# A hybrid attention and SSM layer in float32 on one core: the second half's output projection as seven block products, with weight sums and a scaled input made on GpSimd

## The chip, the cores and the metric

The kernel runs on one core of a Trainium2 chip. The metric is the device time of one execution in microseconds, as a median over runs: 2883.91 us over 3 runs (2882.71 to 2888.22) for the kernel before.

## The reference

A layer takes x (1 x 2048 x 2048, float32) and computes, cut to what matters:

```
h = rms_norm(x, norm_w)
q, k, v, z_attn, u, z_ssm = split(h @ w_in)            # 1024, 256, 256, 1024, 1024, 1024 columns
o_attn = sliding_window_attention(q, k, v, sinks) * silu(z_attn)   # window 128, 16 heads, 4 kv heads
y = gelu(s5_ssm(u, ...)); y = y * sigmoid(y @ w_glu + b_glu)
o_ssm = y * silu(z_ssm)
merged = concat(rms_norm(o_attn, attn_out_norm_w), rms_norm(o_ssm, ssm_out_norm_w))
out = x + merged @ w_out                               # w_out is 2048 x 2048
```

## The kernel before

Every large matrix product is done in three float32r matmuls: each operand is split into a high part (a cast on ScalarE) and a low part (a subtraction on VectorE), and high x high, high x low and low x high are summed in PSUM. The sequence is worked in two halves of 1024 tokens (HT). The activations of a half lie transposed in SBUF as 16 pairs of tiles xh0 to xh15 and xl0 to xl15 (128 x 1024). Weights come through a pool of three buffers each: wr (as loaded, 256 KB), wh and wl (its parts).

The panels are of two kinds. panel_feat (matmul at L331, 512 columns wide, 24 matmuls per weight unit) makes u, z_attn and z_ssm; panel_tok (L349, 256 columns, 48 matmuls per unit) makes q, k, v and the first half's output projection. A third, out_wide (L966), makes the second half's output projection: for four groups of 512 output columns it runs over the attention half and then the SSM half of the 2048 inputs, 8 weight units each, with 8 token tiles and 3 matmuls per tile, 1536 matmuls of 512 columns in all. The row scales of the two norms (ra, rss) are applied per token when PSUM is read out.

The order of the work is written as Python generators: weave runs a list of panels and draws a number of steps of a side generator between them. In turn:

- first u panels of half 0, then u, k, v, q and z_attn of half 0 (6, 6 and 8 panels, 104 weight units), woven with setup_all: rope tables, row statistics of half 1 (x_stats), and ssm_setup, whose last part fills four tables Ct and St on VectorE, one per step, in the pool "tb";
- z_ssm of half 0, then x_later, which loads x of half 1, scales it by the row scale (spread over columns by spread, a set of small matmuls at L281) and by norm_w, and splits it; then u of half 1; woven with attention of half 0 (attend_all, attend: 16 pairs of 128-query blocks, two passes of two heads in each block);
- z_attn, q, k, v, z_ssm of half 1 woven with the SSM itself (ssm_pairs);
- glu of half 0, the output projection of half 0 (out_panel) woven with attention of half 1, glu of half 1 with tail_attn at its side (loads the attention output, splits it, sums its squares), and out_wide.

The steps give a program order; the instruction scheduler of the framework then sets the order on each engine by its own estimate of times and by priorities. All bulk transfers are issued from one queue, SyncE's (SP). That queue is in order too: a store that waits for an engine holds back every load behind it. The staged tiles oa, ob, sz, xq, xr and zt share four buffers of 512 KB.

In attend, a row of scores holds 256 keys of two blocks; only 128 of them are in the window, and they are folded into one 128-wide tile by a mask. The probabilities ph and pl (high and low part, transposed) are multiplied by two masks sel (previous block and own block) into pm, and four matmuls (L562) of pm against the value blocks give the output. The masks of ph run on GpSimd (POOL), those of pl on VectorE.

Of the kernel before, what the change touches and what calls it, by code (L numbers as in the profile page):

```python
# [20 lines left out]
P = 128  # L21
# [20 lines left out]
class Hymba:  # L42
    def __init__(self, ctx, tc, a, out, dbg):
# [25 lines left out]
        self.QS = d("QS", [SEQ, 1024])  # L69
        self.xh, self.xl = [None] * NK, [None] * NK  # L70
# [83 lines left out]
    def consts(self):  # L154
# [11 lines left out]
        self.sel = c.tile([P, 2, P], F32, tag="sel", name="sel")  # L166
        nc.gpsimd.memset(self.sel, 1.0)
        nc.gpsimd.affine_select(out=self.sel[:, 0], in_=self.sel[:, 0], pattern=[[-1, P]],
                                compare_op=ALU.is_gt, fill=0.0, base=0, channel_multiplier=1)
        nc.gpsimd.affine_select(out=self.sel[:, 1], in_=self.sel[:, 1], pattern=[[1, P]],  # L170
# [126 lines left out]
    def x_later(self, half, pool):  # L297

        nc = self.nc
        rb = pool.tile([P, HT], F32, tag="rb", name="rb")  # L300
        self.spread(self.rstd[:, half * 8:half * 8 + 8], rb, pool)
        for k in range(NK):
            x = self.stage("xq")
            self.ld.dma_start(x, self.a["xT"][k * P:(k + 1) * P, half * HT:half * HT + HT])
# [204 lines left out]
    def attend(self, pool, half, g, bq0, kst, vst, zT, qst):  # L509
        nc = self.nc  # L510
        oT = pool.tile([P, 2, 256], F32, tag="oT", name="oT", bufs=2)
        for bq in range(bq0, bq0 + 2):
# [3 lines left out]
            for hp in range(2):  # L516
# [18 lines left out]
                for h in range(2):  # L535
                    self.stt(negm[:, h:h + 1], mx[:, h:h + 1], nrs[:, h:h + 1], nsk[:, h:h + 1], ALU.mult, ALU.min)
# [7 lines left out]
                self.tt(sm, sm, bc(den.unsqueeze(2), (P, 2, P)), ALU.mult)  # L544
# [8 lines left out]
                if b:  # L553
                    pm = pool.tile([P, 2, 2, 256], F32R, tag="pm", name="pm", bufs=2)
                    for i, (pp, eng) in enumerate(((ph, nc.gpsimd), (pl, nc.vector))):
                        for kb in range(2):
                            self.tt(pm[:, i, kb].rearrange("p (h q) -> p h q", h=2), pp.bitcast(F32).rearrange("p (h q) -> p h q", h=2),
                                    bc(self.sel[:, kb].unsqueeze(1), (P, 2, P)), ALU.mult,
                                    eng)
                    for i in range(2):  # L560
                        for kb in range(2):
                            nc.tensor.matmul(po, vst[:, blk + kb, :], pm[:, i, kb], start=(i == 0 and kb == 0),  # L562
                                             stop=(i == 1 and kb == 1))
# [9 lines left out]
            if blk:  # L573
                self.tt(oT, oT, zT, ALU.mult)
                t0 = (b - 1) * P
                self.st.dma_start(self.OA[g * 256:g * 256 + 256, t0:t0 + 256].rearrange("(c p) t -> p c t", p=P), oT)
# [3 lines left out]
    def ssm_setup(self):  # L580
# [162 lines left out]
        with ExitStack() as es:  # L743
            pool = es.enter_context(self.tc.tile_pool(name="tb", bufs=1))
            for bt in range(4):
# [22 lines left out]
                yield  # L768
# [119 lines left out]

    def glu_in(self, half, pool, k0):
# [13 lines left out]
    def glu(self, half, pool, yin, side, k0):  # L903
# [26 lines left out]
        for _ in side:  # L930
            pass
        for m in range(8):
# [23 lines left out]

    def out_wide(self, n):

        nc = self.nc
        for i, k0 in enumerate((0, 8)):  # L960
            ps = [self.psg() if t < 4 else self.psa() for t in range(8)]
            for k in range(8):
                hi, lo = self.w_unit(self.a["w_out"], i * 1024 + k * P, 1, n * 512, 512)
# [172 lines left out]
```

## Time and profile before

| | |
|---|---|
| median of 3 runs | 2883.91 us |
| the profiled execution | 2888.56 us |
| its span on the core | 2886.8 us, mean granted TensorE clock 0.992 |
| TensorE matmuls | 2801.0 us busy (97%), 16992 |
| VectorE, ScalarE, GpSimd | 1897.9, 961.3, 205.0 us busy |

A span is the time from the first to the last instruction on the core. The busy time of TensorE is the union of its matmuls; as they overlap, the pace of a stretch is better read as its length divided by its matmuls. Times of stages below are microseconds from the start of the span.

### The profile page before, as it was taken

To read this page: it belongs to the slowest core of one execution; us is meant where nothing else is said; L and a number is where in the kernel's file an instruction comes from. 1 tells how busy PE (TensorE), PEld (TensorE's weight loads), DVE (VectorE), ACT (ScalarE), POOL (GpSimd) and SP (SyncE) were. 2 spreads that over 40 slices of the span, in tenths; PEclk is the share of its full clock that TensorE was granted. 3 is DMA by queue.
4 is the path that set the end of the run, shared out by engine and by line. 5 is a ranking of instruction groups with operands and counts; after the bars stand their busy time and mean duration, and the time that the engine had idled before them with its cause. 6 is when DMAs were issued, how large, how long until landed. Compare 5 with 4: busy or idle time off the path is not lost.

```text
span 2886.8 us, 45269 instructions
## 1 busy us (share of the span) xinstructions
PE 2801.0 (97%) x16992; PEld 2502.2 (87%) x16992; DVE 1897.9 (66%) x4419; ACT 961.3 (33%) x2089; POOL 205.0 (7%) x341
## 2 busy tenths in 40 slices
PE   6989999989999899999999999998999999999999
PEld 5879999878888688888999988878999999778887
DVE  6682746856773976677679985378999884842222
ACT  6421212134442543333323332345444433521110
POOL 0000000001110112000000000000222220000000
PEclk9999999999999999999999999999999999999999
DMA  5842536553332532544355555343444436333321
GB/s 175 237 117 69 158 92 168 142 142 112 94 115 75 183 115 84 159 144 146 120 156 148 154 156 145 101 138 96 136 143 124 124 106 186 107 104 106 106 78 57
DMA packets 421290, 369.34 MB, mean 128 GB/s; under 512 B 53200, under 2 KB 377296, under 8 KB 421072
## 3 DMA queue, kind: packets, MB, share of 16 engines
q1 hardware_dynamic: 419008, 366.45, 42.9%
q8 instruction: 134, 2.20, 0.3%
q14 instruction: 84, 0.69, 0.1%
q10 hardware_dynamic: 2064, 0.01, 0.0%
HBM read 271.03 MB, written 99.55 MB: 128 GB/s over the span
## 4 chain that ended last, share of the span: by engine, by line
PE 81%; DVE 9%; DMA 6%; issue 2%; ACT 1%; SPq 1%; ACTq 0%; DVEq 0%; POOL 0%; POOLq 0%
PE psg L331 31%; PE psg L349 30%; PE psg L966 6%; PE pss L966 3%; DMA oa<-OA 2%; PE pso L562 2%; PE pss L522 2%; PE pst L966 2%; PE pso L966 1%; DVE ml L93 1%; DVE yg L84 1%; PE pst L547 1%; PE pss L797 1%; DVE wl L84 1%; DVE accs L84 1%
## 5 line engine op out<-in xcount | busy, mean ns | idle before, releaser
L84 DVE TENSOR_TENSOR wl<-wr,wh 128x512 fp32r<-128x512 f32 x456 | 314.6, 690 | 539.6 <-ACT wh L317 530.4
L317 ACT CAST wh<-wr 128x512 fp32r<-128x512 f32 x456 | 282.6, 620 | 1028.3 <-PE psg L331 331.6
L331 PE MATMUL psg<-xl,wh 128*128 128x512 f32 x1536 | 495.3, 395 | 5.2 <-DVE xl L84 5.2
L331 PE MATMUL psg<-xh,wl 128*128 128x512 f32 x1536 | 493.1, 394 | 4.8 <-DVE wl L84 4.7
L331 PE MATMUL psg<-xh,wh 128*128 128x512 f32 x1536 | 492.1, 395 | 3.0 <-ACT wh L317 2.4
L349 PE MATMUL psg<-wh,xh 128*128 128x256 f32 x1536 | 434.2, 284 | 1.8 <-ACT rx L395 1.8
L349 PE MATMUL psg<-wl,xh 128*128 128x256 f32 x1536 | 435.1, 284 | 0.3 <-DVE wl L84 0.3
L349 PE MATMUL psg<-wh,xl 128*128 128x256 f32 x1536 | 433.5, 284 | 0.0
L331 PEld LDWEIGHTS psg<-xl,wh 128*128 128x128 f32 x1536 | 287.9, 189 | 63.7 <-DVE xl L84 7.2
L331 PEld LDWEIGHTS psg<-xh,wl 128*128 128x128 f32 x1536 | 287.5, 189 | 63.0 <-DVE wl L84 6.6
L331 PEld LDWEIGHTS psg<-xh,wh 128*128 128x128 f32 x1536 | 288.0, 190 | 60.8 <-ACT wh L317 3.3
L349 PE MATMUL psg<-wh,mh 128*128 128x256 f32 x1024 | 289.5, 286 | 8.6 <-ACT tt L914 7.7
L349 PEld LDWEIGHTS psg<-wh,xh 128*128 128x128 f32 x1536 | 293.8, 192 | 2.1 <-ACT rx L395 2.0
L349 PEld LDWEIGHTS psg<-wl,xh 128*128 128x128 f32 x1536 | 294.3, 192 | 0.7 <-DVE wl L84 0.7
L349 PEld LDWEIGHTS psg<-wh,xl 128*128 128x128 f32 x1536 | 293.5, 192 | 0.0
L349 PE MATMUL psg<-wl,mh 128*128 128x256 f32 x1024 | 289.7, 284 | 0.7 <-DVE wl L84 0.7
L349 PE MATMUL psg<-wh,ml 128*128 128x256 f32 x1024 | 288.4, 285 | 0.0
L84 POOL TENSOR_TENSOR pm<-ph,sel 128x256 fp32r<-128x256 f32 x240 | 193.1, 825 | 957.6 <-ACT ph L550 612.9
L349 PEld LDWEIGHTS psg<-wh,mh 128*128 128x128 f32 x1024 | 194.7, 191 | 9.4 <-ACT tt L914 7.9
L349 PEld LDWEIGHTS psg<-wl,mh 128*128 128x128 f32 x1024 | 195.9, 191 | 0.9 <-DVE wl L84 0.9
L349 PEld LDWEIGHTS psg<-wh,ml 128*128 128x128 f32 x1024 | 194.7, 191 | 0.0
L539 ACT ACTIVATE sm<-pss,mx,rs 128x128 f32<-128x128 f32 x240 | 108.3, 458 | 93.6 <-DVE mx L93 87.7
(396 smaller groups left out, 4606.6 us busy)
## 6 DMA issues: line engine op xcount, KB each, us to landing
wr<-in_w_in_dram SPq DMA_DIRECT2D x296, 256.0 KB
wr<-in_w_out_dram SPq DMA_DIRECT2D x128, 256.0 KB
tb<-TCS SPq DMA_DIRECT2D x64, 256.0 KB
xr<-in_x_dram SPq DMA_DIRECT2D x64, 256.0 KB
out_dram<-xr SPq DMA_DIRECT2D x64, 256.0 KB
raw<-MBC SPq DMA_DIRECT2D x32, 384.0 KB
kst<-KK SPq DMA_DIRECT2D x56, 192.0 KB
xst<-in_x_dram SPq DMA_DIRECT2D x16, 512.0 KB
```

Source lines behind the costliest of these rows:

```text
L84: (eng or self.nc.vector).tensor_tensor(out=out, in0=a, in1=b, op=op)
L93: self.nc.vector.scalar_tensor_tensor(out=out, in0=a, scalar=s, in1=b, op0=op0, op1=op1)
L317: nc.scalar.copy(hi, raw)
L331: nc.tensor.matmul(ps[t], wt[:, kk, :], xx[k][:, t * 512:(t + 1) * 512], start=(k == 0 and i == 0), stop=(k == nkc - 1 and i == 2))
L349: nc.tensor.matmul(o, xx[k][:, sl], wt[:, kk, :], start=(k == 0 and i == 0 and t % 2 == 0), stop=(k == nkc - 1 and i == 2), skip_group_che ...
L522: nc.tensor.matmul(ps[:, h * 256:h * 256 + 256], qst[:, bq % 2, hp * 2 + h, :], kst[:, i, ksl], start=(h == 0 and i == 0), stop=(i == 1), ...
L539: nc.scalar.activation(sm[:, h, :], sc[:, h, :], AF.Exp, scale=rs[:, h:h + 1], bias=negm[:, h:h + 1], accum_out=den[:, h:h + 1])
L547: nc.tensor.transpose(pt[:, h * P:(h + 1) * P], sm[:, h, :], self.ident)
L562: nc.tensor.matmul(po, vst[:, blk + kb, :], pm[:, i, kb], start=(i == 0 and kb == 0), stop=(i == 1 and kb == 1))
L797: nc.tensor.matmul(o, m[:, g, 0:128], u[:, g, 384:640], start=(g == 0 and i == 0), stop=(i == 2), skip_group_check=True)
L966: nc.tensor.matmul(ps[t], xx[k0 + k][:, t * P:(t + 1) * P], wt[:, 0, :], start=(k == 0 and j == 0), stop=(k == 7 and j == 2))
```

## The change

The second half's output projection is written as a product of 2 x 2 blocks: the activations are cut by tokens (512 + 512) and by inputs (attention, SSM), w_out by inputs and by output columns. The eight block products (each 512 x 1024 by 1024 x 1024) become seven, by Winograd's form of Strassen's scheme: product runs one of them in two groups of 512 output columns with 8 weight units of 12 matmuls each. It needs sums of weight blocks T1 to T4 (made by out_sums on POOL during ssm_setup's table part and stored to DRAM as WT), sums and differences of activation blocks (form_first, form_s2, form_s1 and others, drawn as side generators inside the products), and sums of products, which the functions e1 to e7 make when PSUM is read out.

Since blocks are added before they are multiplied, the norms' row scales must be in the activations. For attention, the sum of squares is gathered in attend (asq), and attn_scale multiplies the output by the spread row scale on POOL, through DRAM (OAN); for the SSM, form_ssm does it. x_later's row scale is applied on POOL beside the tables too (x_scaled, through DRAM as XN). ssm_setup yields four times per table in place of once, and setup_all is woven in 42 steps in place of 30.

In attend the value difference dv of neighbouring blocks is made on POOL, so that one mask is left: the output is vst of the previous block times p, plus dv times the masked p, again four matmuls. The division by the denominator moves from VectorE to ScalarE, and two small operations of VectorE do for two heads at once. Attention of half 1 is spread over 0.7 of its panels in place of 0.5.

```
     def ssm_setup(self):
+            sums, xs = self.out_sums(pool), self.x_scaled(pool, 1)
             for bt in range(4):
...
-                yield
+                for _ in range(4):
+                    next(sums, None)
+                    next(xs, None)
+                    yield
...
+    def out_sums(self, pool):
+        for k in range(8):
+            x, y = (pool.tile([P, HT], F32, tag=f"ws{i}", name=f"ws{i}") for i in range(2))
+            get = lambda t, q: self.ld.dma_start(t, self.w_block(q, k, 0, 1024))
+            put = lambda i, t: self.st.dma_start(self.WT[i, k], t)
+            get(x, 1)
+            get(y, 0)
+            self.tt(x, x, y, ALU.subtract, g)
+            put(0, x)
+            get(y, 3)
+            self.tt(y, y, x, ALU.subtract, g)
+            put(1, y)
+            yield
+            get(x, 2)
+            self.tt(x, y, x, ALU.subtract, g)
+            put(3, x)
+            get(x, 1)
+            get(y, 3)
+            self.tt(y, y, x, ALU.subtract, g)
+            put(2, y)
+            yield
+    def x_scaled(self, pool, half):
...
+        for k in range(NK):
+            x = pool.tile([P, HT], F32, tag="xs", name="xs", bufs=2)
+            self.ld.dma_start(x, self.a["xT"][k * P:(k + 1) * P, half * HT:half * HT + HT])
+            self.tt(x, x, rb, ALU.mult, self.nc.gpsimd)
+            self.st.dma_start(self.XN[k], x)
+            yield
     def x_later(self):
-            self.stt(x, x, self.nw[:, k:k + 1], rb, ALU.mult, ALU.mult)
-            nc.scalar.copy(self.xh[k], x)
-            self.tt(self.xl[k], x, self.xh[k].bitcast(F32), ALU.subtract)
+            nc.scalar.activation(self.xh[k], x, AF.Copy, scale=w)
+            self.stt(self.xl[k], x, w, self.xh[k].bitcast(F32), ALU.mult, ALU.subtract)
     def attend(self, pool, half, g, bq0, kst, vst, zT, qst):
-                self.tt(sm, sm, bc(den.unsqueeze(2), (P, 2, P)), ALU.mult)
+                for h in range(2):
+                    nc.scalar.activation(sm[:, h, :], sm[:, h, :], AF.Copy, scale=den[:, h:h + 1])
...
+                if half:
+                    nc.scalar.activation(sq, oT, AF.Square)
+                    acc = self.asq[:, t0 - HT:t0 - HT + 256]
...
+    def attn_scale(self, pool):
+        for k in range(8):
+            o = pool.tile([P, HT], F32, tag="on", name="on")
+            self.ld.dma_start(o, self.OA[k * P:(k + 1) * P, HT:SEQ])
+            self.tt(o, o, self.rba, ALU.mult, self.nc.gpsimd)
+            self.st.dma_start(self.OAN[k], o)
+            yield
+    def product(self, slot, q, evac, *sides):
+        for n in range(2):
+            ps = [self.psg() if n == 0 else self.psa() for t in range(4)]
+            for k in range(8):
...
+                for t in range(4):
+                    sl = slice(o + t * P, o + t * P + P)
+                    for j, (xx, wt) in enumerate(((self.sh[c], hi), (self.sh[c], lo), (self.sl[c], hi))):
+                        nc.tensor.matmul(ps[t], xx[:, sl], wt, start=(k == 0 and j == 0), stop=(k == 7 and j == 2))
...
+        self.product(0, B11, e1, (ssm, 6, 4))
+        self.product(1, T3, e7, (ssm, 4, 0), (s2, 3, 10))
+        self.product(2, B21, e2, (s2, 5, 0))
+        self.product(0, T2, e6, (s1, 8, 0))
+        self.product(1, T1, e5, (s4, 8, 0))
+        self.product(2, B22, e3, (a22, 8, 0))
+        self.product(0, T4, e4)
     def run(self):
-        self.weave(U(0, 2) + QKV(0) + Z(0, C_ZA, self.ZA), self.setup_all(), 30, 0.0, 0.95, PU)
+        self.weave(U(0, 2) + QKV(0) + Z(0, C_ZA, self.ZA), self.setup_all(), 42, 0.0, 0.95, PU)
...
-            self.weave(o0[:-1], self.attend_all(pool, 1), 33, 0.0, 0.5, PA)
+            self.weave(o0[:-1], self.attend_all(pool, 1), 33, 0.0, 0.7, PA)
...
-            self.glu(1, pool, yin, self.tail_attn(1, pool, 0), 8)
+            self.weave(o0[-1:], self.attn_scale(pool), 8, 0.0, 1.0, 0)
+            self.glu(1, pool, yin, self.form_first(), 8)
+            self.strassen_out(pool)
```

On SyncE's queue (SP), in the z_attn panels of half 0, a row is a transfer that it issues; wr is a weight unit of a panel, ZA and OA the stores of z and of attention outputs, kst, vst, q and zT the loads of attention. Before:

```order
L382 DMA ZA<-zt 128x1024
L314 DMA wr<-in_w_in_dram 128x4x128 x2
L486 DMA q_7791<-QS 128x2x256
L484 DMA vst<-VS 128x3x128
L488 DMA zT<-ZA 128x2x256
L576 DMA OA<-oT 128x2x256
L314 DMA wr<-in_w_in_dram 128x4x128 x2
L382 DMA ZA<-zt 128x1024
```

and now, where ws are the two tiles of out_sums and WT its stores:

```order
L323 DMA wr<-in_w_in_dram 128x4x128
L1020 DMA WT<-ws_6459 128x1024
L1019 DMA ws_6639<-in_w_out_dram 128x1024
L323 DMA wr<-in_w_in_dram 128x4x128
L1019 DMA ws_6640<-in_w_out_dram 128x1024
L323 DMA wr<-in_w_in_dram 128x4x128
L391 DMA ZA<-zt 128x1024
L1020 DMA WT<-ws_6639 128x1024
L1019 DMA ws_6640<-in_w_out_dram 128x1024
L323 DMA wr<-in_w_in_dram 128x4x128
L1020 DMA WT<-ws_6640 128x1024
```

The transfers of attention have moved behind the last store of WT, since attention's tiles take the memory of the pool "tb"; in their place stand out_sums' loads and stores, and each store WT waits for POOL. From the first load of k = 3 to the last store of k = 7 the queue holds 29 weight units (7, 5, 6, 5 and 6).

On VectorE (DVE), where x of half 1 is split beside attention of half 0. Before:

```order
L84 TENSOR_TENSOR xl_9600<-xq,xh_9599 128x1024
L93 SCALAR_TENSOR_TENSOR xq<-xq,nw,rb 128x1024
L84 TENSOR_TENSOR mx<-mx,nsink 128x2
L84 TENSOR_TENSOR sm<-sm,mx 128x256
L84 TENSOR_TENSOR xl_9602<-xq,xh_9601 128x1024
```

and now:

```order
L96 SCALAR_TENSOR_TENSOR xl_9857<-xq,nw,xh_9856 128x1024
L554 TENSOR_REDUCE mx<-pss 128x2
L87 TENSOR_TENSOR pm<-pl,sel 128x256
L554 TENSOR_REDUCE mx<-pss 128x2
L87 TENSOR_TENSOR mx<-mx,nrs 128x2 x2
```

One of the two long operations per tile of x is gone, and the product sm by the denominator with it.

## Rows read from the trace of the kernel before

**Rows 1.** The page: busy time of the engines, and the chain that ended last, by engine

```profile
PE 2801.0 (97%) x16992; PEld 2502.2 (87%) x16992; DVE 1897.9 (66%) x4419; ACT 961.3 (33%) x2089; POOL 205.0 (7%) x341
...
PE 81%; DVE 9%; DMA 6%; issue 2%; ACT 1%; SPq 1%; ACTq 0%; DVEq 0%; POOL 0%; POOLq 0%
```

**Rows 2.** Stretches: length, then busy us (count) by engine, clock, DMA share, GB/s

```profile
300.00:450.00 150.00, 149.36 (x1266) 149.18 (x1265) 91.41 (x179) 34.29 (x66) 0.00 (x0) 1.00 0.42 122
450.00:540.00 90.00, 87.92 (x692) 85.74 (x691) 62.47 (x198) 17.22 (x27) 0.60 (x6) 1.00 0.62 166
540.00:620.00 80.00, 67.79 (x296) 55.04 (x295) 54.45 (x131) 13.95 (x27) 0.54 (x3) 0.96 0.60 167
...
940.00:1020.00 80.00, 68.67 (x314) 54.60 (x313) 75.50 (x158) 41.46 (x93) 14.02 (x13) 0.94 0.56 171
2420.00:2520.00 100.00, 96.07 (x453) 79.59 (x452) 71.12 (x88) 51.09 (x73) 0.00 (x0) 1.00 0.45 137
2520.00:2560.00 40.00, 33.31 (x136) 26.07 (x136) 29.30 (x53) 17.92 (x23) 0.00 (x0) 0.87 0.26 80
2560.00:2880.00 320.00, 320.00 (x1413) 265.00 (x1412) 77.90 (x117) 35.55 (x57) 0.00 (x0) 1.00 0.29 86
```

**Rows 3.** Waits of PE: line, what it waited for, us in total, times, longest

```profile
PE pst L492 <- DMA q<-QS: 7.5, 1, 7.5
...
PE psg L331 <- DVE xl L84: 5.2, 5, 1.4
...
PE psg L966 <- ACT wh L317: 3.4, 1, 3.4
```

**Rows 4.** Line L281, the matmuls of spread: ns min/median/max, first and last start

```profile
L281 PE MATMUL pss<-diag,ones x8: 271/275/377, 944.5 to 947.2; 128*128 128x128 f32 x8
```

**Rows 5.** Groups of instructions by line and form: busy us, mean ns, idle before

```profile
L84 DVE TENSOR_TENSOR wl<-wr,wh 128x512 fp32r<-128x512 f32 x456 | 314.6, 690 | 539.6 <-ACT wh L317 530.4 <-DMA xst<-in_x_dram 4.3 <-DMA wr<-in_w_in_dram 2.3
...
L317 ACT CAST wh<-wr 128x512 fp32r<-128x512 f32 x456 | 282.6, 620 | 1028.3 <-PE psg L331 331.6 <-PE pst L966 284.4 <-PE psg L349 277.9
...
L93 DVE SCALAR_TENSOR_TENSOR ml<-yg,sow,mh 128x512 fp32r<-128x512 f32 x32 | 36.5, 1197 | 0.0
...
L93 DVE SCALAR_TENSOR_TENSOR xq<-xq,nw,rb 128x1024 f32<-128x1024 f32 x16 | 21.2, 1333 | 0.4 <-DMA xq<-in_xT_dram 0.4
...
L93 DVE SCALAR_TENSOR_TENSOR yl<-yg,yh 128x1024 fp32r<-128x1024 f32 x16 | 19.5, 1222 | 8.6 <-ACT yh L898 8.2
L84 DVE TENSOR_TENSOR xl<-xq,xh 128x1024 fp32r<-128x1024 f32 x16 | 19.3, 1211 | 0.0
...
L93 DVE SCALAR_TENSOR_TENSOR xr<-psg,rar,xr 128x512 f32<-128x512 f32 x16 | 11.3, 745 | 19.1 <-PE psg L966 19.1
```

**Rows 6.** The chain that ended last, its end: start, us, what

```profile
2877.76 5.51 DVE xr L93 x8
```

**Rows 7.** Instructions on tile pm: ns min/median/max, first and last start

```profile
L84 POOL TENSOR_TENSOR pm<-ph,sel x240: 724/742/2300, 639.9 to 2365.9; 128x256 fp32r<-128x256 f32 x120
L84 DVE TENSOR_TENSOR pm<-pl,sel x240: 397/418/1020, 642.0 to 2366.2; 128x256 fp32r<-128x256 f32 x120
```

**Rows 8.** Timeline at 1941: start, length, instruction, idle before and its releaser

```profile
1941.30 0.32 SPq L879 DMA_DIRECT2D oa<-OA  x1
...
1946.03 0.72 ACT L869 ACTIVATE mh<-oa,aow 128x512 fp32r<-128x512 f32 x1 [2.03 <-DMA oa<-OA]
```

**Rows 9.** Timeline at 1307: a store of 256 KB, and what waited for its landing

```profile
1307.39 0.36 SPq L838 DMA_DIRECT2D YS<-y  x1
...
1311.77 0.10 POOL L817 MEMSET H<- 128x2 f32 x1 [17.09 <-DMA YS<-y]
```

**Rows 10.** Waits of the SP queue: line, what it waited for, us in total, times, longest

```profile
SPq L314 <- DVE wl L84: 988.9, 287, 10.8
```

**Rows 11.** Timeline at 78: a load of 512 KB among others, and its reader

```profile
77.81 0.91 SPq L292 DMA_DIRECT2D xst<-in_x_dram  x2
...
84.92 1.06 ACT L293 ACTIVATE xst<-xst 128x1024 f32<-128x1024 f32 x1 [6.34 <-DMA xst<-in_x_dram]
```

More of the change, by code (lines that the diff above doesn't have):

```diff
@@ new lines, in strassen_out, with part, rows, final @@
+    def strassen_out(self, pool):
+        nc = self.nc
+        acc = {}
+        def part(n, c, t):
+            i = (8 * c + 4 * n + t) // 2
+            if i not in acc:
+                acc[i] = self.xt.tile([P, HT], F32, tag=f"x{'hl'[i // 4]}{12 + i % 4}", name=f"ac{i}")
+            return acc[i][:, (t % 2) * 512:(t % 2) * 512 + 512]
+        e = lambda n, t: part(n, 0, t)
+        v = lambda n, t: part(n, 1, t)
+        def rows(y, r, c, n, t):
+            r0 = HT + r * 512 + t * P
+            return y[0, r0:r0 + 2 * P, c * 1024 + n * 512:c * 1024 + n * 512 + 512].rearrange("(t p) c -> p t c", p=P)
+        xs = {}
+        def final(r, c, n, t, ps, base, keep, op=ALU.add):
+            if t % 2 == 0:
+                x = self.stage("xr").rearrange("p (t c) -> p t c", t=2)
+                xs[0] = x, (self.stage("xo").rearrange("p (t c) -> p t c", t=2) if keep else x)
+            x, o = xs[0]
+            v = o[:, t % 2] if keep else base
+            self.tt(v, base, ps, op)
+            if t % 2 == 0:
+                self.ld.dma_start(x, rows(self.a["x"], r, c, n, t))
+            self.tt(x[:, t % 2], x[:, t % 2], v, ALU.add, nc.gpsimd)
+            if t % 2:
+                self.st.dma_start(rows(self.out, r, c, n, t - 1), x)
+        def e1(n, t, ps):
+            nc.scalar.copy(e(n, t), ps)
+        def e7(n, t, ps):
+            self.tt(v(n, t), e(n, t), ps, ALU.add)
+        def e2(n, t, ps):
+            final(0, 0, n, t, ps, e(n, t), True)
+        def e6(n, t, ps):
+            self.tt(e(n, t), e(n, t), ps, ALU.add)
+            self.tt(v(n, t), v(n, t), ps, ALU.add)
+        def e5(n, t, ps):
+            self.tt(e(n, t), e(n, t), ps, ALU.add)
+            final(1, 1, n, t, ps, v(n, t), True)
+        def e3(n, t, ps):
+            final(0, 1, n, t, ps, e(n, t), False)
+        def e4(n, t, ps):
+            final(1, 0, n, t, ps, v(n, t), False, ALU.subtract)
+        def ssm_side():
+            self.rss = self.row_scale(pool, self.gacc, 0.125, "rs")
+            yield
+            self.spread(self.rss, self.rbs, pool)
+            yield
+            yield from self.form_ssm()
+        B11, B12, B21, B22, T1, T2, T3, T4 = range(8)
+        ssm, s2, s1 = ssm_side(), self.form_s2(), self.form_s1()
+        s4, a22 = self.form_view(2, 0), self.form_view(0, 1)
+        self.product(0, B11, e1, (ssm, 6, 4))
[5 more added lines that the diff above has]
+        self.product(0, T4, e4)
@@ L931, in glu @@
             pass
+        if half:
+            self.yg, self.gacc = yg, acc
+            return
         for m in range(8):
```

179 lines of the change are left out of this document (131 added, 48 removed).

## The prediction

> **What bounds the kernel now.** I read the page first: TensorE (PE) is busy 97% of the span and holds 81% of the chain that ended last [rows 1]. So a change pays where it takes matmuls away or closes one of the few gaps. Where those gaps are, a table of stretches shows [rows 2]. out_wide (2560 to 2880) has none: 320 us for 1413 recorded matmuls, 0.2265 us each, at full clock, with VectorE (DVE) busy a quarter of the time. The gaps lie in three other stretches. At 540 to 620 PE lacks 12.2 us, and its granted clock averages 0.96 of 2.4 GHz, which loses another 3.2; PE waits there for a load of q [rows 3], late behind the table stores on the SP queue. At 940 to 1020 it lacks 11.3 and, at 0.94, another 4.8; DVE is busy 75.5 of the 80 us, and PE waits for xl, the low part of x [rows 3]. At 2520 to 2560, between glu and out_wide, it lacks 6.7 and, at 0.87, another 5.2; PE waits there for a weight's cast [rows 3]. The sum below is made against the profiled execution, 2888.6 us; the median of the runs is 4.7 lower.
>
> **The change, part by part.**
>
> *Matmuls.* out_wide's 1536 become 7 x 2 x 8 x 4 x 3 = 1344 of the same shape: 192 x 0.2265 = **-43.5** [rows 2]. Two more spreads of 8 small matmuls cost 16 x 0.275 = **+4.4** [rows 4]. Attention still issues four matmuls per pair of heads; PE is the bound there, so what DVE is spared (half its masks, one product) counts as nothing, and ScalarE, busy a third of the span, covers the scaling it takes over.
>
> *The products.* A weight unit now lasts 12 matmuls, 2.72 us, and asks DVE for 0.69 and ScalarE for 0.62 [rows 5], which fits. The sides are tighter. The second product is the worst: 16 weights (11.0 us), 8 readings of PSUM at 0.745 (6.0), four steps of form_ssm (one strided operation over 1024 columns, 2 x 1.2, and one over 512, 1.2: 14.4) and three of form_s2 (1.2 + 0.75 + 0.69 + 1.2: 11.5), with the strided price from ml<-yg [rows 5]. That is 42.9 us of DVE in 43.5 us of PE. Three raw and three split weight tiles are the cover; bounds 0 and +11 (the weights unhidden); I take **+4**.
>
> *The end.* Before, the last bank was followed by DVE alone [rows 6]. Now POOL adds x after DVE, four times some 1.5 us (2 x 0.742) [rows 7] against four of 0.745: **+3**.
>
> *Weight sums on SP and POOL.* This is the main cost. Each k of out_sums is a chain: load, operation, load, operation, load, operation, store that must land, load, operation, store that must land before the next k loads. A 512 KB load takes 4.7 us from issue to its reader [rows 8], a 256 KB store 4.4 [rows 9]. No row has POOL on 128 x 1024; four times the median of 128 x 256 is 2.97 [rows 7]. So a k takes 4 x 4.73 + 4 x 2.97 + 2 x 4.4 = 39.6 us, five of them 198. But the queue's order puts only 29 weight units, 29 x 24 x 0.2265 = 158 us of PE, among the last five k, and it is in order: each store WT holds the wr behind it. The excess is 40 us. Against it stands the lead of the weights: SP waits 989 us in all for free weight buffers [rows 10], so it runs about five units ahead, 27.2 - 4.7 - 0.6 - 0.7 = 21. Left: **+19**. Bounds: 0 (the lead covers all), and +73 with the slowest load at hand, 7.1 us [rows 11], and POOL at its mean of 4 x 0.825. The Trainium skill (GPSIMD Engine Reference, Elementwise — side-by-side cycle accounting) gives 4497 ns for an add of 2048 columns, so an estimate of 2.25 us here; by it the term would be about +5. No row here shows that shape.
>
> *Tables in 16 steps.* The table operations of DVE spread over more weight units, so most of the gap at 540 to 620 should close; the first loads of attention still queue behind the last sums, so I leave a late q: **-9**, bounds -15 and 0.
>
> *x of half 1.* Per tile DVE did 1.333 + 1.211 us; now one operation, like yl at 1.222 [rows 5]: 21 us less of the 75.5. The waits for xl should go, those of attention stay: **-12**, bounds -16 and 0. The 16 POOL operations of x_scaled run beside the sums, in the first k, where the order has 9 to 14 units per k, and cost nothing there; without that cover they are in the +73.
>
> *attn_scale.* A load, an operation and a store per k, 12.1 us; 7 of them are 85 us against 12 glu units, 65, in the queue. The lead covers that 20 just: **+4**, bounds -4 (glu now spares DVE the sum of squares) and +20.
>
> *Glu to projection.* The 16 strided splits of the SSM output, 1.2 us each on DVE [rows 5], no longer stand between glu and the first weights: **-8**, bounds -12 and 0.
>
> Sum: -43.5 + 4.4 + 4 + 3 + 19 - 9 - 12 + 4 - 8 = -38. From 2888.6 that is 2850.5, and as a median 4.7 less: **2846**.
>
> **The rivals.**
>
> *A. As summed*, 2846 (own range 2822 to 2870).
>
> *B. Every new chain is covered*: no +19, +4, +4, and x's whole 16 regained: 2815. For it speaks that SP spends a third of the span waiting for buffers [rows 10]; against it, that a POOL operation must end before the queue moves on.
>
> *C. The sums' chain paces the kernel*, slower. Transfers grow: 112 loads and stores of 512 KB, 59 MB, are added to a stretch that already moves 166 GB/s [rows 2]. With 7.1 us per load the chain is 50.4 per k, 252 in five, +73; gaps of that size drop the clock as at 540 to 620, some 3.2 us each, five of them: 2846 - 19 + 73 + 16 = 2916. It decides from a load of about 6.6 us on, at which the 38 is used up (20 x 1.9).
>
> *D. POOL and DVE block each other.* On pm, POOL's longest is 2300 ns against a median of 742, DVE's 1020 against 418 [rows 7], so one does hold up the other at times. If each of the 48 operations on 128 x 1024 held DVE for its 2.97 us, that is 143 us on top of DVE's 208 in 320 us from 300 to 620 [rows 2]: 351, and DVE is the bound by some 30, part of it at the same time as the sums' stalls: +20, so 2866. The Trainium skill (SBUF — State Buffer, Who interferes with whom) says this: a GpSimd operation and a VectorE operation with two SBUF inputs exclude each other for a whole instruction. By that rule D would be sure; the trace bears it out only in part, since wl, with both inputs in SBUF, has a mean of 690 over all 456, attention included [rows 5].
>
> *E. The products are not shorter than out_wide*, because DVE paces the sides: the 43.5 is lost, 2890, on the edge of a loss. Against it: only the second product comes near its limit.
>
> **How the numbers follow.** A 0.50, B 0.18, D 0.10, E 0.07, C 0.15. The forecast is A's. The range leaves out some of B's and most of C's: 2803 to 2895. A measurement tells 0.2%, 5.8 us. Faster are A, B and D, 0.78; E divides between same and slower, so same 0.04; slower 0.18.
>
> **What would show it.** Right: the last 300 us hold 1344 matmuls at about 0.227 us with no gap, PE's wait for xl is gone, and the only new gaps, some 3 us each, lie in the z_attn panels before attention of half 0, where SP waits for POOL's sums and PE for wl or wh. Wrong: gaps of 5 us and more there with the clock below 1 (C), DVE's operations on SBUF well over 0.69 us while POOL runs (D), or products of more than 45 us (E). If the sums' loads land in under 4 us, B.

## The result, and the profile after

The changed kernel takes **2970.84 us** (median of 4 runs, 2967.43 to 2973.16) against 2883.86 before: ratio **1.0298**, 95% interval 1.0280 to 1.0316. The forecast was 2846, with a range of 2803 to 2895. It is slower by 87 us where 38 less were expected. The profiled execution took 2968.68 us, its span 2967.0.

The page of the changed kernel answers to [rows 1] with the first two lines (busy time by engine, the chain that ended last by engine), and to the first of [rows 5] with the third (busy us, mean ns, idle before).

```profile
PE 2791.3 (94%) x16832; PEld 2490.1 (84%) x16832; DVE 1924.0 (65%) x4277; ACT 1104.2 (37%) x2469; POOL 401.1 (14%) x440
...
PE 59%; DVE 7%; DMA 4%; issue 2%; ACT 2%; POOL 1%; SPq 0%; POOLq 0%; ACTq 0%; DVEq 0%
...
L87 DVE TENSOR_TENSOR wl<-wr,wh 128x512 fp32r<-128x512 f32 x504 | 373.0, 743 | 556.5 <-ACT wh L326 421.9
```

PE has 160 matmuls less, and it is idle for 176 us of the span in place of 86. Its share of the chain fell from 81% to 59%, and DVE's wl now takes 743 ns in the mean where it took 690. PE's waits in the whole span, the longest groups (line, what it waited for, us in total, times, longest):

```profile
PE pss L1063 <- DVE wl L87: 25.9, 5, 14.6
PE pst L501 <- DMA zT<-ZA: 23.1, 1, 23.1
PE pss L270 <- DVE x L91: 21.9, 4, 11.5
PE psg L340 <- ACT tt L1171: 18.8, 10, 4.3
PE psg L358 <- DVE wl L87: 18.1, 9, 3.6
PE psg L340 <- ACT wh L326: 9.8, 10, 2.0
PE psg L358 <- ACT tt L1171: 7.8, 1, 7.8
PE pss L460 <- DVE rx L87: 5.7, 1, 5.7
PE psg L1063 <- DVE wl L87: 5.1, 3, 2.7
```

The waits for x and the 7.8 for tt stood in the kernel before as well (21.9 and 7.7 us there), and 8.6 of the 18.8. Where the others lie, a table of stretches shows (columns as in [rows 2], where POOL's busy time is the one ahead of the clock):

```profile
400.00:500.00 100.00, 86.67 (x678) 85.65 (x677) 78.09 (x177) 12.52 (x20) 51.69 (x17) 0.95 0.76 254
500.00:600.00 100.00, 87.77 (x553) 80.50 (x552) 78.63 (x150) 17.56 (x28) 43.56 (x16) 0.93 0.81 262
700.00:800.00 100.00, 68.07 (x272) 51.88 (x270) 17.81 (x19) 11.25 (x20) 24.94 (x14) 0.87 0.66 199
1520.00:1540.00 20.00, 8.73 (x41) 7.85 (x42) 17.76 (x36) 6.72 (x12) 0.20 (x2) 0.57 0.56 184
2500.00:2560.00 60.00, 49.97 (x204) 39.91 (x203) 34.16 (x33) 19.40 (x30) 19.23 (x10) 0.94 0.70 232
2640.00:2680.00 40.00, 19.12 (x69) 14.79 (x68) 38.99 (x35) 15.94 (x20) 0.00 (x0) 0.74 0.15 46
```

The granted clock averages 0.976 of 2.4 GHz over the span (0.992 before); it is low in the stretches above in which PE stands idle.

To see what each stage lost, I took the matmuls of the panels in their order and read off when the same one (the 2282nd of 256 columns, say) starts in both kernels. A lag that grows within a stage is that stage's loss. Attention's own matmuls stand at other places in the changed order, so neighbouring rows can trade a few us. The table has the lag against the kernel before in us, for the changed kernel and for six of the experiments below:

| up to | before, at | after | e1 | e2 | e4 | e7 | e13 | e12 |
|---|---|---|---|---|---|---|---|---|
| the end of the q panels, half 0 | 528 | 33 | 33 | 39 | 1 | 0 | 29 | 3 |
| the end of z_attn, half 0 | 737 | 13 | 12 | 31 | 0 | -1 | 14 | -19 |
| two panels of z_ssm, half 0 | 796 | 41 | 42 | 32 | 0 | -1 | 15 | -19 |
| the first matmul behind z_ssm, half 0 | 955 | 44 | 45 | 35 | 5 | 4 | 18 | -15 |
| the end of the split of x, half 1 | 1020 | 34 | 35 | 23 | -6 | -7 | 7 | -26 |
| the end of z_attn, half 1 | 1361 | 40 | 43 | 12 | -2 | -3 | 7 | -26 |
| the end of the k and v panels, half 1 | 1506 | 65 | 67 | 7 | 9 | 9 | 6 | -29 |
| the end of SSM and glu, half 0 | 1952 | 67 | 68 | 7 | 10 | 11 | 6 | -29 |
| the end of the projection, half 0 | 2416 | 72 | 74 | 13 | 18 | 22 | 13 | -20 |
| the end of glu, half 1 | 2515 | 87 | 89 | 29 | 35 | 26 | 27 | -19 |
| the end of the span | 2887 | 80 | 65 | 21 | 28 | -3 | 18 | -45 |

So the changed kernel is 40 us late by the end of z_attn of half 1. It loses 33 us in the q panels, gains 20 in z_attn of half 0 (where the kernel before has its own gap at 540 to 620, [rows 2], and already runs a part of attention), loses 27 for the late start of attention (its first scores stand at 809 in place of 614), gains 10 at the split of x and loses 9 in the panels around it. Then it loses 25 in the k and v panels of half 1, 20 of them at one place, some 7 by the end of the first half's projection and 15 in glu of half 1. The products give back 7.

### The profile page after: what moved, and what is told of

Same layout as the page of the kernel before. It is cut to its first block, busy times and chain, and to the rows that moved or that the text cites. A ratio compares the mean times of both kernels' runs of the same rounds, so it can differ in the third digit from the quotient of the medians.

```text
span 2967.0 us, 45801 instructions
## 1 busy us (share of the span) xinstructions
PE 2791.3 (94%) x16832; PEld 2490.1 (84%) x16832; DVE 1924.0 (65%) x4277; ACT 1104.2 (37%) x2469; POOL 401.1 (14%) x440
## 4 chain that ended last, share of the span: by engine, by line
PE 59%; DVE 7%; DMA 4%; issue 2%; ACT 2%; POOL 1%; SPq 0%; POOLq 0%; ACTq 0%; DVEq 0%
PE psg L340 22%; PE psg L358 21%; PE psg L1063 4%; PE pss L542 2%; PE pss L1063 2%; DMA oa<-OA 1%; DVE yg L87 1%; DMA ob<-OAN 1%; PE pso L1063 1%; PE pso L582 1%; PE pst L568 1%; PE pso L580 1%; PE pst L1063 1%; DVE wl L87 1%; DVE yg L96 1%
## 5 line engine op out<-in xcount | busy, mean ns | idle before, releaser
L87 DVE TENSOR_TENSOR wl<-wr,wh 128x512 fp32r<-128x512 f32 x504 | 373.0, 743 | 556.5 <-ACT wh L326 421.9
L326 ACT CAST wh<-wr 128x512 fp32r<-128x512 f32 x392 | 242.3, 619 | 773.0 <-PE psg L340 266.6
L340 PE MATMUL psg<-xh,wh 128*128 128x512 f32 x1536 | 492.4, 395 | 10.3 <-ACT wh L326 9.8
L87 POOL TENSOR_TENSOR pm<-ph,sel 128x256 fp32r<-128x256 f32 x120 | 92.7, 772 | 446.4 <-ACT ph L571 426.0
L1057 ACT CAST wh<-wr 128x512 fp32r<-128x512 f32 x112 | 69.7, 626 | 180.1 <-PE psg L1063 81.2
```

The source lines that it names most:

```text
L87: (eng or self.nc.vector).tensor_tensor(out=out, in0=a, in1=b, op=op)
L326: nc.scalar.copy(hi, raw)
L340: nc.tensor.matmul(ps[t], wt[:, kk, :], xx[k][:, t * 512:(t + 1) * 512], start=(k == 0 and i == 0), stop=(k == nkc - 1 and i == 2))
L1057: nc.scalar.copy(hi, raw)
```

## The experiments

All medians stand beside runs of the kernel before on the same chip; the ratios are against those.

**1. The order of DVE's work in the products.** In the trace of the changed kernel the eight scalings of form_ssm stand in one row on DVE (timeline: start, length, instruction):

```profile
2630.35 0.69 DVE L87 TENSOR_TENSOR wl<-wr,wh 128x512 fp32r<-128x512 f32 x1 [2.03 <-ACT wh L1057]
...
2641.01 16.09 DVE L96 SCALAR_TENSOR_TENSOR yg<-yg,sow,rbs 128x1024 f32<-128x1024 f32 x8 [2.84 <-ACT rbs L283]
2657.01 1.15 DVE L96 SCALAR_TENSOR_TENSOR ob<-ob,aow,yg 128x512 f32<-128x512 f32 x1
2658.05 0.69 DVE L87 TENSOR_TENSOR wl<-wr,wh 128x512 fp32r<-128x512 f32 x1
```

e1_pinned makes each scaling read the weight of the step at which it is drawn:

```
             y = self.yg[k].rearrange("p (t c) -> p t c", t=8)
-            self.stt(y, y, self.sow[:, k:k + 1], self.rbs..., ALU.mult, ALU.mult)
+            self.stt(self.sop[:, k:k + 1], self.now.bitcast(F32)[:, 0:1], 0.0, self.sow[:, k:k + 1], ALU.mult, ALU.add)
+            self.stt(y, y, self.sop[:, k:k + 1], self.rbs..., ALU.mult, ALU.mult)
```

> The changed kernel with one thing more: each of the eight scalings of the SSM output (form_ssm, 128x1024, 2.0 us each on DVE) reads the low part of the weight unit of the step at which it is drawn, by a one-column operation, so that the scheduler can't set all eight in one piece. Theory (order on DVE): in the changed kernel the eight stand together, 16.1 us from 2641, ahead of the weights' low parts; PE waits 25.9 us in five for wl there, and the clock falls. Spread, the stretch should lose 20 us or more of it: 2940 to 2952 against 2971, and no wait of PE for wl above 5 us in the products. Rival (DVE is full): the first products ask DVE for as much as PE takes, so the same work in another order only moves the waits: within 8 us of 2971, PE's waits for wl in sum as before.

Measured: 2952.28, ratio 1.0227 (1.0204 to 1.0249). Waits of PE from 2600 on in e1:

```profile
PE psg L1065 <- DVE wl L87: 7.7, 6, 2.7
PE pss L1065 <- DVE wl L87: 7.1, 6, 3.6
```

The waits for wl fell from 31.0 us to 14.8, the longest from 14.6 to 3.6, and the lag changes only behind glu. The theory holds, at the edge of its range: 19 us were a matter of order alone. 14.8 us of waits stay, 8.7 of them in the fourth product. Measured from the first matmul of a product to that of the next, the first product takes 53.0 us in place of 75.4, the second 48.7 in place of 43.5 (its share of the scalings had run in the first), and the fourth 58.4 as against 58.1. The second in e1, then the fourth in the changed kernel:

```profile
2660.70:2709.40 48.70, 44.77 (x194) 35.72 (x193) 44.57 (x55) 19.05 (x30) 0.00 (x0) 1.00 0.32 98
```

```profile
2769.70:2827.80 58.10, 48.99 (x194) 38.87 (x193) 48.52 (x61) 23.08 (x35) 6.13 (x4) 0.91 0.45 145
```

In the fourth, DVE does nine of the splits of SSM blocks (fl from yg) that the program draws beside the fifth and sixth products, besides the product's own side work. No run here moves them.

**2. The sums, their queue, their engine.** e2_no_sums leaves out_sums out; e3_pool_queue issues the loads and stores of the sums and of the scaled x from GpSimd's queue; e4_sums_dve moves their 48 operations to DVE.

```
 e2:  -            sums, xs = self.out_sums(pool), self.x_scaled(pool, 1)
      +            xs = self.x_scaled(pool, 1)
      -        if q > 3:
      -            return self.WT[q - 4, k, :, c0:c0 + n]
      +        q %= 4
 e3:  -            get = lambda t, q: self.ld.dma_start(t, self.w_block(q, k, 0, 1024))
      +            get = lambda t, q: g.dma_start(t, self.w_block(q, k, 0, 1024))
 e4:  -        g = nc.gpsimd
      +        g = nc.vector
      -            self.tt(x, x, rb, ALU.mult, self.nc.gpsimd)
      +            self.tt(x, x, rb, ALU.mult)
```

> The changed kernel without the weight sums: out_sums is left out, and the products that read T1 to T4 read plain blocks of w_out of the same size; x_scaled stays. Theory (the sums pace the q panels and make attention late): by the pace of the matmuls the q panels lose 37 us against the kernel before, and the wait of 23 us for zT comes because attention's tiles take the memory of the sums. Without them most of both goes: 2915 to 2940. Rival (not the sums but what stands beside them): the scaling of x on POOL and the tables in 16 steps hold the queue by themselves: 2955 or more, and the gaps between 400 and 600 stay.

> The changed kernel with the loads and stores of out_sums and of x_scaled issued from GpSimd's queue in place of SyncE's; the same bytes and the same operations. Theory (an in-order queue behind a slow engine): SP stands still behind a store that waits for POOL, up to 13.9 us at 424, and the weights stand behind it. With a queue of its own this goes: 2930 to 2945, the q panels (400 to 590) lose less than 10 us, and POOL's operations are as slow as before beside the tables. Rival (POOL and DVE exclude each other, and the transfers crowd the rings): the panels stay slow with the other queue: 2960 or more, up to 2990 if POOL's descriptor work collides with DVE.

> The changed kernel with the operations of out_sums and x_scaled (48 on 128x1024) on DVE in place of POOL; queue and bytes as they are. On DVE one takes some 1.2 us, 58 us in all. Theory (POOL is shut out by DVE): POOL's operation took 2.4 us alone and 17.4 in a stretch in which DVE ran table operations without a gap, and SP waited for it; on DVE the operation stands in DVE's own order and takes 1.2, so the queue is held less: 2940 to 2960. Rival 1 (the transfers pace the chain): within 8 us of 2971. Rival 2 (DVE becomes the bound in the q panels, its 62 of 90 us plus 58 over 200): 2975 to 2995.

Measured: e2 2909.17, ratio 1.0071 (1.0055 to 1.0088). e3 2978.64, 1.0314 (1.0298 to 1.0331). e4 2915.33, 1.0094 (1.0078 to 1.0111).

e2 comes out 6 us faster than its theory's range, but not where the theory said: the q panels lose 39 us **without any sum**. The 16 operations of x_scaled on POOL are enough for that. What the sums cost lies behind: attention starts on time in e2 (first scores at 602), and the lag falls to 12. e3 refutes SyncE's queue as the cause in the q panels: with its own queue for POOL's work they still lose 36 us. e4, 25 us faster than its theory's range, removes the loss in the q panels altogether (33 to 1) though it puts 59 us more on DVE. So it is POOL and DVE together. The timeline of the changed kernel shows how, both ways:

```profile
412.08 2.40 POOL L87 TENSOR_TENSOR ws<-ws,ws 128x1024 f32<-128x1024 f32 x1 [2.06 <-DMA ws<-in_w_out_dram]
412.13 2.39 DVE L87 TENSOR_TENSOR tu<-St,us 128x32 f32<-128x32 f32 x1
414.45 0.18 DVE L87 TENSOR_TENSOR tv<-Ct,us 128x32 f32<-128x32 f32 x1
...
420.78 17.44 POOL L87 TENSOR_TENSOR xs<-xs,rb 128x1024 f32<-128x1024 f32 x1 [6.30 <-DMA xs<-in_xT_dram]
424.35 0.37 SPq L440 DMA_DIRECT2D QS<-rx  x1
427.86 1.21 DVE L87 TENSOR_TENSOR Ct<-Ct,uc 128x1024 f32<-128x1024 f32 x1
...
435.27 0.68 DVE L87 TENSOR_TENSOR wl<-wr,wh 128x512 fp32r<-128x512 f32 x1
438.24 0.33 SPq L306 DMA_DIRECT2D XN<-xs  x1
```

A DVE operation of 0.18 us that starts beside POOL's lasts as long as POOL's (2.39). A POOL operation of some 2.4 us that meets a row of DVE operations without a gap ends one such length after the row does (the row at 435.95, POOL at 438.22, 17.44 in all), and SyncE issues nothing from 424.35 to 438.24, since the store XN stands at its head.

**3. The exclusion by itself.** e10_pool_dose is the kernel before with 16 additions on POOL that nobody waits for (the tables' two small memsets go to DVE, so that nothing stands behind the additions):

```
+                for _ in range(4):
+                    self.tt(dz, dz, dz, ALU.add, nc.gpsimd)
                 yield
```

> The kernel before, and 16 additions of 128x1024 on POOL beside the tables, on a tile that nothing else reads or writes: no transfer, no queue and no other engine waits for them; the tables' two small memsets go from POOL to DVE so that nothing stands behind the additions. Theory (each engine shuts the other out for whole operations): POOL alone needs 16 x 2.4 = 38 us; DVE's operations of 0.17 us among them take up to 2.4, DVE loses up to 38 us in a stretch where it is busy two thirds, and the kernel is 8 to 25 us slower. Rival (only the queue behind POOL cost time): within 4 us of the kernel before.

Measured: 2916.92, ratio 1.0096 (1.0079 to 1.0112): 29 us slower, 1.8 per addition of 1.95, a little above the theory's range. 25 of the 29 are lost in the q panels by the lag of the matmuls. The rival is out. Timeline of e10:

```profile
462.50 28.70 POOL L84 TENSOR_TENSOR dz<-dz 128x1024 f32<-128x1024 f32 x14
...
468.39 0.21 DVE L84 TENSOR_TENSOR Ct<-Ct,uc 128x64 f32<-128x64 f32 x1
468.53 1.95 DVE L84 TENSOR_TENSOR tu<-St,us 128x64 f32<-128x64 f32 x1
470.40 0.21 DVE L84 TENSOR_TENSOR tv<-Ct,us 128x64 f32<-128x64 f32 x1
470.53 1.91 DVE L84 TENSOR_TENSOR St<-St,uc 128x64 f32<-128x64 f32 x1
472.37 0.21 DVE L84 TENSOR_TENSOR Ct<-Ct,tu 128x64 f32<-128x64 f32 x1
472.50 1.91 DVE L84 TENSOR_TENSOR St<-St,tv 128x64 f32<-128x64 f32 x1
...
487.07 2.38 DVE L84 TENSOR_TENSOR wl<-wr,wh 128x512 fp32r<-128x512 f32 x1
...
489.50 0.58 PE L349 MATMUL psg<-wl,xh 128*128 128x256 f32 x1 [20.32 <-DVE wl L84]
```

The engines take turns: every other table operation, 0.21 us by itself, is held for a whole addition, and the weight's wl stands in that row and takes 2.38. PE waits 20.3 us.

**4. What is left of the sums: a chain.** e9_dve_poolq and e11_four_loads start from e7 (part 5 below: every large new operation on DVE, scalings spread). e13_four_pool is the changed kernel with the four-tile form alone. To make room for the four tiles, e11 and e13 put the tables' second scratch tile on the first one's buffer.

```
 e9:   -            get = lambda t, q: self.ld.dma_start(t, ...)
       +            get = lambda t, q: nc.gpsimd.dma_start(t, ...)
 e11:  +            w = [pool.tile([P, HT], F32, tag=f"ws{q}", name=f"ws{q}") for q in range(4)]
       +            for q in (1, 0, 3, 2):
       +                self.ld.dma_start(w[q], self.w_block(q, k, 0, 1024))
       +            yield
       +            self.tt(w[0], w[1], w[0], ALU.subtract)
       +            self.tt(w[1], w[3], w[1], ALU.subtract)
       +            self.tt(w[3], w[3], w[0], ALU.subtract)
       +            self.tt(w[2], w[3], w[2], ALU.subtract)
       +            for i, q in ((0, 0), (2, 1), (1, 3), (3, 2)):
       +                self.st.dma_start(self.WT[i, k], w[q])
 e13:  the same on after, each subtraction with nc.gpsimd
```

> As the run with no large operation left on POOL (2886), and the loads and stores of out_sums issued from GpSimd's queue, which has nothing else to do there. Theory (what is left of the sums' chain): between 590 and 750 SyncE stood 90.8 us in 17 behind stores of WT that waited for DVE's operation and its load, and PE waited 16.2 us in nine for wl and 8.7 for zT. With the chain on its own queue the weights run ahead: 2864 to 2876. Rival (the transfers themselves crowd the rings, 200 to 230 GB/s there): within 5 us of 2886.

> As the run with no large operation left on POOL (2886), and out_sums written with four tiles: per k all four blocks are loaded first, one step ahead, then the four subtractions in place and the four stores; 32 loads in place of 48. (The tables' second scratch tile is dropped to make room.) Theory (what is left of the sums is a chain: each load waits for an operation and a store waits on SyncE for both, 90.8 us in 17 between 580 and 750, and on the run with GpSimd's queue DVE itself stood 131.5 us in 17 before ws): with the loads ahead neither waits; the z_attn panels lose nothing and attention starts on time: 2862 to 2874. Rival (the bytes crowd the weights out): within 5 us of 2886.

> The changed kernel with the four-tile form of out_sums alone, its subtractions left on POOL (as the scaling of x is). This sets the chain of the sums (loads that wait for operations, stores that wait for both) against the mutual exclusion of POOL and DVE. Theory (both cost, at different places: the exclusion the 33 us of the q panels, the chain what follows): the q panels still lose 25 to 45 us against the kernel before, the wait for zT goes, 2930 to 2955. Rival 1 (the chain was all): the q panels lose less than 10, 2900 to 2915. Rival 2 (the exclusion was all, and denser operations of POOL make it worse): 2965 to 2990.

Measured: e9 2922.13, ratio 1.0121 (1.0106 to 1.0136), 36 us slower than e7, which neither view expected. e11 2847.33, 0.9856 (0.9839 to 0.9872), 15 us faster than its theory's range. e13 2906.20, 1.0064 (1.0047 to 1.0081).

The waits of DVE from 580 to 820, in e7 and then in e9, say a part of why:

```profile
DVE ws L87 <- DMA ws<-in_w_out_dram: 87.4, 14, 8.6
```

```profile
DVE ws L87 <- DMA ws<-in_w_out_dram: 131.5, 17, 9.8
```

SyncE no longer stands behind the stores of WT, but a subtraction that waits for its load holds every wl behind it on DVE, now for 131.5 us. PE's waits for wl in that stretch rise from 16.2 us to 28.1, and the chain ends 48 us later, attention with it (first scores at 791 in place of 741). By the lag against e7, the 10 us that e9 loses in the q panels are made up in z_attn; 18 are lost at the late start of attention and 12 at the k panel of half 1. e11 takes the wait itself away, by loading a step ahead, and gains 39 us on e7. It also loads 16 blocks less, but the bytes were not the limit: where e7 moved 215 GB/s with gaps in PE, e11 begins with 306 and has none:

```profile
580.00:750.00 170.00, 144.97 (x603) 116.19 (x602) 51.24 (x74) 25.61 (x51) 2.92 (x7) 0.93 0.70 215
```

```profile
580.00:620.00 40.00, 40.00 (x179) 33.10 (x178) 20.74 (x24) 6.07 (x11) 0.00 (x0) 1.00 0.95 306
```

e13 shows both causes at their two places, as its theory said, though the chain was worth more than the theory gave it: the q panels still lose 29 us, but the lag is 7 by the end of z_attn of half 1, and its time falls into the range of the rival that put all on the chain. In the same run POOL costs nothing where DVE is light (e13's stretches, columns as above):

```profile
400.00:500.00 100.00, 82.24 (x625) 81.43 (x624) 95.18 (x175) 12.74 (x20) 48.69 (x22) 0.88 0.78 257
500.00:600.00 100.00, 93.85 (x634) 86.99 (x634) 88.61 (x151) 19.01 (x30) 48.05 (x18) 0.97 0.88 297
600.00:700.00 100.00, 100.00 (x465) 83.36 (x464) 38.28 (x82) 29.86 (x81) 38.89 (x23) 1.00 0.74 255
```

Over the whole run, e4 gains 55 us and e11 another 39 on e7; with the chain first, e13 gains 65, and 30 of the 94 are left for the exclusion. These sums hold more than the setup stage, since 13 to 20 us of e4's and e13's gains are the stall at the k panel. Up to two panels of z_ssm, the lags (41 in after, 0 in e4, 15 in e13, -20 in e11) give the exclusion 35 to 40 us and the chain, attention's late start included, 20 to 26. How they split depends on which is removed first.

**5. The rest of POOL's work.** e5_pin_dve joins e1 and e4; e6_side_dve moves attn_scale's product and form_first's difference to DVE, e7_all_dve also the additions of x in final (in each, the engine argument is dropped from a self.tt).

> The two remedies that were measured alone, together: the weight sums and the scaling of x on DVE in place of POOL, and the scalings of the SSM output spread. Theory (two causes at two places that don't touch): the gains add up, 2971 - 55 - 19 = 2897, 2890 to 2904. Rival (they share something, such as the total load of DVE): 2905 to 2915.

> As the run before it, and attn_scale's multiplication (eight of 128x1024) and form_first's subtraction (eight of 128x512) on DVE in place of POOL as well; both stand beside glu of half 1. Theory (POOL's operations hold DVE there: in the changed kernel DVE took 2.77 for an operation of 0.74, 3.15 for one of 1.1, and PE waited for tt 14.2 us in six): 8 to 16 us less than the run before it. Rival (the longer chain of loads and stores on SyncE's queue delays the sides, not POOL): within 4 us of the run before it.

> As the run before it, and the 32 additions of x in final (128x512) on DVE too, so that no large operation of the change is left on POOL. Theory (POOL's 1.46 us each hold DVE in the products that write out): 4 to 10 us less, and a shorter end. Rival (DVE is near its limit in these products, 32 more operations of 0.69 push it over): 2 to 10 us more.

Measured: e5 2900.86, ratio 1.0043 (1.0029 to 1.0058), inside the theory's range. e6 2888.16, 1.0000 (0.9991 to 1.0010). e7 2886.32, 0.9993 (0.9984 to 1.0002). The gains of e1 and e4 add up within their uncertainty. e6 confirms the exclusion in glu of half 1: it gains 13 us on e5, and PE's waits for tt there fall from 15.9 us to 2.8. The changed kernel's timeline has it:

```profile
2519.64 2.35 POOL L87 TENSOR_TENSOR on<-on,rba 128x1024 f32<-128x1024 f32 x1 [0.67 <-POOL ob L87]
2519.77 2.77 DVE L96 SCALAR_TENSOR_TENSOR fl<-ob,aow,fh 128x512 fp32r<-128x512 f32 x1 [0.24 <-ACT fh L944]
...
2525.65 0.79 PE L340 MATMUL psg<-yh,wh 128*128 128x512 f32 x1 [4.27 <-ACT tt L1171]
...
2526.46 0.74 DVE L96 SCALAR_TENSOR_TENSOR fl<-ob,aow,fh 128x512 fp32r<-128x512 f32 x1
```

The next operation of the same line and form, with POOL idle, takes 0.74. e7's further step is too small to tell from none.

**6. Attention alone.** e8_att_only puts the changed attend into the kernel before, without its sum of squares.

```
+        dv = pool.tile([P, 2, P], F32R, tag="dv", name="dv", bufs=2)
...
-                        for kb in range(2):
-                            self.tt(pm[:, i, kb]..., bc(self.sel[:, kb]...), ALU.mult, eng)
+                        self.tt(pm[:, i]..., bc(self.sel...), ALU.mult, eng)
```

> The kernel before with the changed attention alone (value differences on POOL, one mask, the division on ScalarE), without its sum of squares. The prediction counted this part as nothing: 2878 to 2890 against 2884. Rival (the new POOL operations on the values hold DVE, which stands on the path where attention runs beside projections): 2892 to 2900. Rival 2 (DVE is relieved where it is busy 75 of 80 us, beside the split of x): 2868 to 2877.

Measured: 2881.82, ratio 0.9978 (0.9969 to 0.9988), inside the first range, but 6 us below the kernel before on the same chip (2887.86), which is that range's edge. The interval lies wholly below 1. By the lag, 7 us are gained at the split of x of half 1, so the relief of DVE that the second rival spoke of is there, at the size of its smallest value.

**7. A version that beats both.** e12_early_scale spreads attn_scale in e11 over two panels:

```
-            self.weave(o0[:-1], self.attend_all(pool, 1), 33, 0.0, 0.7, PA)
+            self.weave(o0[:-2], self.attend_all(pool, 1), 33, 0.0, 0.8, PA)
...
-            self.weave(o0[-1:], self.attn_scale(pool), 8, 0.0, 1.0, 0)
+            self.weave(o0[-2:], self.attn_scale(pool), 8, 0.0, 0.9, 0)
```

> As the run before it, and attn_scale spread over the last two panels of the first half's projection in place of one, attention over 0.8 of the six before. Theory (eight multiplications of 1.22 us on DVE in one panel stand before the reading of PSUM: PE waited 5.4 us in two for xr there): 3 to 8 us less than the run before it. Rival (attention becomes denser by that and pays it back): within 3 us of it, or slower.

Measured: **2843.04**, ratio 0.9839 (0.9824 to 0.9854), 4 us below e11, on the edge of what the intervals separate. Its stretches:

```profile
400.00:500.00 100.00, 99.50 (x829) 99.30 (x829) 89.31 (x204) 19.90 (x31) 0.45 (x4) 1.00 1.00 352
500.00:600.00 100.00, 100.00 (x574) 88.53 (x574) 85.56 (x180) 18.19 (x30) 0.22 (x2) 1.00 0.96 327
700.00:800.00 100.00, 100.00 (x511) 84.86 (x510) 54.80 (x167) 48.01 (x143) 13.59 (x23) 1.00 0.38 114
```

DVE is busier than in the changed kernel (89 and 86 of 100 us against 78 and 79), the DMA engines have a share of 1.00 and 0.96, and PE has no gap to speak of. So it was neither DVE's work nor the bandwidth that held PE there before. The products still take 334 us from first to last, where seven of 43.5 would take 305: the fourth alone takes 55.6, with DVE busy 47.0.

## Why the prediction was wrong, step by step

**The step that failed** is the pricing of POOL beside DVE. It shows in three places: the 16 operations of x_scaled "cost nothing", the sums' chain took POOL's 2.97 us as if POOL were free to run, and rival D, which had the mechanism, got +20 us and a chance of 0.10. Measured, the exclusion is 35 to 40 us in the setup stage (part 4) and some 13 in glu (e6). The argument against D was that wl has a mean of 690 ns over all its instructions [rows 5]. That mean could not speak: in the stretches with the tables POOL was busy 0 to 0.6 us [rows 2], and in the whole kernel before only 7 of the 456 wl start while an operation of POOL runs. These 7 take 0.92 us in the mean, the others 0.69. The longest pm of 2300 ns [rows 7] was the row that did speak. The Trainium skill (SBUF — State Buffer, Who interferes with whom) says that a VectorE operation with two SBUF inputs and a GpSimd operation that reads SBUF exclude each other for a whole instruction. The traces agree (2.39 us for an operation of 0.18 on DVE), and POOL's 17.44 for one of 2.4 goes further, since it waited for a whole row of DVE's. By that rule D was the likeliest case.

*Weight sums*, +19 with a range to +73. The chain itself was well reckoned: its last five k take 192 us in the changed kernel where 198 were summed. PE's waits for weights in that stretch are 10.3 us, less than the 19. What the term lacked is what hangs on the chain's end. Removing the chain gains 20 to 26 us in the setup stage with attention's late start, and 39 to 65 over the whole run (part 4). So mechanism C was at work, and in the right place; the term was too small by what stood behind the chain's end.

*Late attention*. Its first loads were known to stand behind the last sums, and the tables' term keeps a late q within its -9, but no price is given for attention as a whole. PE waited 23.1 us for zT, with the clock at 0.87 in that stretch.

*The k panel of half 1*, +20, was not in the sum at all. The change redraws the order far from its place. Between the two groups of transposes of k, PE's panel matmuls (the stretch in after, then the same place in before, that line alone; the first two columns are PE and its weight loads):

```profile
1519.70:1535.00 15.30, 0.00 (x0) 0.00 (x0) 0.56 0.61 195
```

```profile
1437.00:1453.00 16.00, 14.36 (x117) 14.20 (x118) 1.00 0.40 130
```

Where the order leaves PE 117 matmuls there, the rope operations of DVE are hidden; where it leaves none, PE waits for each. At that place the lag grows by 20 us in after, e1 and e9, by 39 in e3, by 7 in e4 to e7, and by nothing in e2, e11, e12 and e13. e9 has no operation of out_sums or x_scaled on POOL, so the exclusion isn't what tips the order; what does stays open.

*The products*, -43.5 and +4 for their sides. The count of matmuls is right (160 less in all: 192 less in the products, 32 new ones in spreads, where 16 were counted; the spreads are busy 7.97 us in place of 2.80, near the term's 4.4). DVE's total in the second product was right too, 44.6 us in e1 for the 42.9 of the sum, and tight: it takes 48.7. Two things failed. A total was priced and not an order: eight operations in one piece cost 19 us (e1). And only the second product was said to come near its limit, while the fourth is the longest of those behind the first in every version looked at (58.1 in after, 58.4 in e1, 55.6 in e12). From the end of glu to the end of the span, after takes 7 us less than before, e1 24, e12 27. Rival E was half the truth.

*Tables in 16 steps*, -9: the q panels lose nothing in e4 and e7, and the wait for q is gone, but the gain shows only where the chain is gone too: e12 gains 22 us in z_attn of half 0, some of it because less of attention stands there by then. *x of half 1*, -12: the lag falls by 10 us from the first matmul behind z_ssm to the end of the split, in the changed kernel and in e7 and e12. The size is right, the cause is shared: e8, which has attention's change alone, gains 7 there. *Attention*, 0: off by those 7 us, 6 in the whole of e8. *attn_scale and glu*, +4: wrong by the exclusion, 15 lost in glu of half 1, 13 of it back in e6. *The end*, +3: the last link of after's chain is two additions on POOL of 1.2 us each; e7, without them, can't be told from e6. *Glu to projection*, -8: no run has this part alone.

That e12 lands at 2843, where the sum had 2846, is luck. The sum had this program run with POOL's work as written, and it holds +19 for a chain that e12 no longer has. Against the kernel before on its chip e12 gains 47 us: by the lag, 29 in the first half and the k and v panels of the second, of which 10 go again by the end of glu, and 27 in the products, where the terms -43.5, +4, +3 and -8 make 44.5. What it shows is that seven products do pay once the causes are taken away one by one.

## What to carry to other kernels

An idle GpSimd is not a free engine beside a VectorE that works on two SBUF inputs. Where VectorE stood on the path, a GpSimd operation of 1.95 to 2.4 us on 128x1024 cost 1.4 to 2.4 us here (33 us for the 23 that began in the q panels, 29 for 16 in e10, 39 for 16 in e2); where it was busy 38 of 100 us it cost nothing (e13, 600 to 700). So give it work only where VectorE has real gaps, and before trusting a mean as evidence against contention, see whether the two ever ran together. An operation that waits for a load blocks whatever is behind it, on a queue or on an engine; moving it to another in-order place moved the block (e9), loading a step ahead removed it (e11). And price a side stream by the order in which its operations stand between the critical ones, not by its total.

## What was not expected of the hardware

How long one of the two engines waits for the other was not bounded by the other's single operation. In e10 they took turns; in the changed kernel POOL's operation of 2.4 us lasted 17.44, until DVE's row had ended. DVE's operations follow one another without a gap in both places (each starts some 0.08 us before the last one's end), so what decides between the two isn't shown. And with DVE busy 89 us of 100, the DMA engines at a share of 1.00 and 352 GB/s, PE's matmuls kept their pace (e12, 400 to 500).
